# A narrower scope for the scan's priority, a priority for the split of weights, and two small buffer edits

## The chip, the cores and the metric

The kernel runs on one core of a Trainium2 chip. Its engines are TensorE (PE; the loading of its stationary operand is listed apart as PEld), VectorE (DVE), ScalarE (ACT), GpSimd (POOL) and SyncE (SP), whose queue issues the DMAs here. The metric is the device time of one execution in microseconds: before the change 2582.29 us, the median of three runs (2581.88 to 2584.9).

## The reference, cut to what matters

Two layers over 2048 tokens of width 1024, everything in float32: a Mamba-2 layer (SSD) and a sliding-window attention layer with sinks. Each is norm, one input projection, mixer, gate, one output projection, norm, residual. The part of the Mamba layer that the change touches is the chunked scan, with 8 groups of 4 heads, a state of 128 and chunks of 128 tokens:

```python
seg = a_cs[..., :, None] - a_cs[..., None, :]
decay = jnp.exp(jnp.where(causal, seg, -jnp.inf))
cb = jnp.einsum('bclgn,bcsgn->bcgls', Cc, Bc)
y_diag = jnp.einsum('bcgrls,bcsgrp->bclgrp', cb[:, :, :, None] * decay, x)
states = jnp.einsum('bclgn,bcgrl,bclgrp->bcgrpn', Bc, decay_to_end, x)
...
y_off = jnp.einsum('bclgn,bcgrpn,bcgrl->bclgrp', Cc, h_in, jnp.exp(a_cs))
```

## The kernel before, in words

**Products.** Every large product runs as three matmuls on operands that are split into a rounded high part and the remainder: high·high, low·high and high·low (`mm3`, L88). A block of weights (128 columns, all 1024 rows) is split in `split_w` (L143): a DMA brings `wraw`, ACT copies it to `whi`, POOL subtracts to get `wlo`. Each of the three tiles has two buffers, so the block after next can only be split when the products of an earlier one are done with its buffers. The same function splits the gate weights of the attention layer.

**Stages.** The Mamba layer goes through the tokens in two halves of 1024. In a half, the loop over the 8 groups runs `ssm_proj` (L665): six blocks of weights (B, C, x0, x1, z0, z1), each multiplied with two blocks of 512 tokens, 24 matmuls a product; behind each product ACT evicts it and DVE and ACT apply the convolution and the SiLU. The scan of the group before (`ssm_scan`, L756) is interleaved into these products: `interleave` (L49) advances it in 19 steps over a group. The scan of the half's first group can't start before `dt_proj` (L588) has made the half's tables; it comes with the second group. After the last group the scan runs beside the first pieces of the output projection. Then the output projection, the attention layer (head groups of 4 query heads, two halves of tokens) and its output projection follow.

**The scan.** `stage1` (L770) works on one chunk. PE transposes x and B and multiplies B with C; DVE and ACT make `xd`, `bh`, `bl`, `xw`, `xh`, `xl` (the operands of the state products) and `cbm`, the masked scores; then four ACT Relu and an exponential make the decays `dec` from `ab` (the row sums, broadcast by a DMA), another exponential and a product on POOL turn `ab` into `ce`, and DVE multiplies `dec` by `cbm`. The steps of the scan are: stage1 of chunks 0 and 1, then for each pair of chunks the state products (`sps`) and the carrying of the state, stage1 of the next two chunks, and the output products (`yt`, L847), which read `xd`, `dec`, `ce` and the states.

**The order on the engines.** The program text isn't the order of execution. A planner goes through the instructions with estimated durations and gives each engine, at each moment, the ready instruction that stands first in the text; a tile that has no free buffer makes its first writer not ready. `high_priority(offset=n)` moves the instructions of its block n places forward in this ranking. Each engine then executes its list in that order and waits on semaphores where something isn't there yet. In `stage1` everything after PE's part has an offset of 60.

**Small tensors at the start.** `ssm_consts` (L554) loads the convolution weights, their bias and the gate norm as `rows`, transposes them on PE and scales them into `cw`, `cb` and `gn`. It stands in the text behind the first whole product of B. The ring `px` has four buffers of 128 x 1024 floats; the x tiles of `prep` (L95, four for each block of 512 tokens) and some scratch of `dt_proj` go through it.

Of the kernel before, what the change touches and what calls it, by code (L numbers as in the profile page):

```python
# [11 lines left out]
F32 = mybir.dt.float32  # L12
F32R = mybir.dt.float32r
I32 = mybir.dt.int32
U32 = mybir.dt.uint32
AF = mybir.ActivationFunctionType
ALU = mybir.AluOpType
# [4 lines left out]
P = 128  # L22
T = 2048
D = 1024
# [36 lines left out]
class Trunk:  # L61
# [81 lines left out]
    def split_w(self, src, cols):  # L143

        nc = self.nc
        kt = src.shape[0] // P
        raw = self.wp.tile([P, kt, cols], F32, tag="wr", name="wraw")
        nc.sync.dma_start(raw, src.rearrange("(k p) c -> p k c", p=P))
        hi = self.wp.tile([P, kt, cols], F32R, tag="wh", name="whi")
        nc.scalar.activation(hi, raw, AF.Copy)  # L150
        lo = self.wp.tile([P, kt, cols], F32R, tag="wl", name="wlo")
        nc.gpsimd.tensor_tensor(lo, raw, hi.bitcast(F32), ALU.subtract)  # L152
        return hi, lo

    def rope_tables(self, wp):
# [398 lines left out]
    def ssm_consts(self, pool):  # L554
        nc, io = self.nc, self.io

        def bcast(ap, n, name):
            t = pool.tile([P, n], F32, name=name)
            nc.sync.dma_start(t, ap.partition_broadcast(P))
            return t  # L560

        self.abc = bcast(io["ssm_a_log"][0], NH, "abc")
        nc.scalar.activation(self.abc, self.abc, AF.Exp)
        nc.vector.tensor_scalar(self.abc, self.abc, -1.0, None, ALU.mult)
        self.dtb = bcast(io["ssm_dt_bias"][0], NH, "dtb")
        d = bcast(io["ssm_d"][0], NH, "dall")
        self.dch = pool.tile([P, NH // 2], F32, name="dch")
        d2 = d.rearrange("p (t two) -> p t two", two=2)
        nc.vector.tensor_copy(self.dch[0:64], d2[0:64, :, 0])
        nc.vector.tensor_copy(self.dch[64:P], d2[64:P, :, 1])  # L570

        self.cw = pool.tile([P, 4, 32], F32, name="cw")
        self.cb = pool.tile([P, 32], F32, name="cb")
        rows = pool.tile([P, 2, P], F32, name="rows")
        nc.sync.dma_start(rows[:, 0, :], io["ssm_conv_w"][0].rearrange("k (t p) -> (k t) p", p=P))
        nc.sync.dma_start(rows[0:32, 1, :], io["ssm_conv_b"][0].rearrange("(t p) -> t p", p=P))
        nc.sync.dma_start(rows[32:48, 1, :], io["ssm_gate_norm"][0].rearrange("(t p) -> t p", p=P))
        pt = self.tp.tile([P, P], F32, tag="tr", name="pt")
        nc.tensor.transpose(pt, rows[:, 0, :], self.ident)
        nc.vector.tensor_scalar(self.cw.rearrange("p k t -> p (k t)"), pt, 0.5, None, ALU.mult)  # L580
        pt = self.tp.tile([P, 48], F32, tag="tr", name="pt")
        nc.tensor.transpose(pt, rows[0:48, 1, :], self.ident[0:48, 0:48])
        nc.vector.tensor_scalar(self.cb, pt[:, 0:32], 0.5, None, ALU.mult)
        nc.vector.tensor_scalar(self.gn, pt[:, 32:48], 0.5, None, ALU.mult)
        self.halo = pool.tile([P, 32, 3], F32, name="halo")
        self.hsave = [pool.tile([P, 256], F32, name=f"hsave{g}") for g in range(NG)]
# [169 lines left out]
    def ssm_scan(self, sp, yp, tabs, hf, g, res, yT):  # L756


        nc = self.nc
        dt, acs, cd, w2, atd = (tabs[k] for k in ("dt", "acs", "cd", "w2", "atd"))  # L760
# [9 lines left out]
        def stage1(c):  # L770
            if c > 7:
                return
            ab = abs_[c]
            s, o = divmod(c, 4)
            sl = slice(o * P, (o + 1) * P)
            x0, x1, Bt, Ct = (res[n, s] for n in ("x0", "x1", "B", "C"))
            pt = (yp.tile([P, 4, P], F32, tag="y", name="pt", bufs=2) if c % 2
                  else self.tp.tile([P, 4, P], F32, tag="tr", name="pt"))
            nc.tensor.transpose(pt[:, 0, :], x0[:, sl], self.ident)
            nc.tensor.transpose(pt[:, 1, :], x1[:, sl], self.ident)  # L780
            last = hf == 1 and c == 7
            if not last:
                nc.tensor.transpose(pt[:, 2, :], Bt[:, sl], self.ident)
            nc.tensor.matmul(pt[:, 3, :], Bt[:, sl], Ct[:, sl], start=True, stop=True)
            with self.tc.high_priority(offset=60):
                xv = pt[:, 0:2, :].rearrange("p a (h d) -> p (a h) d", d=64)
                xd = sp.tile([P, 4, 64], F32, tag="xd", name="xd", bufs=4)
                hb = dt[:, c, 4 * g:4 * g + 4].unsqueeze(2).to_broadcast([P, 4, 64])
                nc.vector.tensor_tensor(xd, xv, hb, ALU.mult)
                bx = None  # L790
                if not last:
                    bh = sp.tile([P, P], F32R, tag="bh", name="bh")
                    nc.scalar.activation(bh, pt[:, 2, :], AF.Copy)
                    bl = sp.tile([P, P], F32R, tag="bl", name="bl")
                    nc.vector.tensor_tensor(bl, pt[:, 2, :], bh.bitcast(F32), ALU.subtract)
                    xw = sp.tile([P, 4, 64], F32, tag="xw", name="xw", bufs=1)
                    hb = w2[:, c, 4 * g:4 * g + 4].unsqueeze(2).to_broadcast([P, 4, 64])
                    nc.vector.tensor_tensor(xw, xv, hb, ALU.mult)
                    xf = xw.rearrange("p h d -> p (h d)")
                    xh = sp.tile([P, 256], F32R, tag="xh", name="xh")  # L800
                    nc.scalar.activation(xh, xf, AF.Copy)
                    xl = sp.tile([P, 256], F32R, tag="xl", name="xl")
                    nc.vector.tensor_tensor(xl, xf, xh.bitcast(F32), ALU.subtract)
                    bx = bh, bl, xh, xl
                cbm = sp.tile([P, P], F32, tag="cbm", name="cbm", bufs=1)
                nc.vector.tensor_tensor(cbm, pt[:, 3, :], self.triu, ALU.mult)
                dec = sp.tile([P, 4, P], F32, tag="dec", name="dec", bufs=4)
                for r in range(4):
                    nc.scalar.activation(dec[:, r, :], ab[:, r, :], AF.Relu, scale=-1.0,  # L809
                                         bias=acs[:, c, 4 * g + r:4 * g + r + 1])  # L810
                ce = None
                if not (hf == 0 and c == 0):
                    ce = ab
                    nc.scalar.activation(ce, ab, AF.Exp)  # L814
                    nc.gpsimd.tensor_tensor(ce, ce, Ct[:, sl].unsqueeze(1).to_broadcast([P, 4, P]), ALU.mult)  # L815
                nc.scalar.activation(dec, dec, AF.Exp, scale=-1.0)
                nc.vector.tensor_tensor(dec, dec, cbm.unsqueeze(1).to_broadcast([P, 4, P]), ALU.mult)  # L817
            sts.append((xd, bx, dec, ce))

        def states(c):  # L820
# [54 lines left out]
        for c in range(4):  # L875
            load(c)
        stage1(0)
        yield
        stage1(1)
        yield  # L880
        hprev = self.hsave[g] if hf else None
        hd = decayed(0, hprev)
        yield
        for c in range(0, 8, 2):
            sps = states(c)
            h0 = hprev
            h1, hd = state(c, sps[:, 0, :], hd)
            yield
            hprev, hd = state(c + 1, sps[:, 1, :], hd)
            stage1(c + 2)  # L890
            yield
            stage1(c + 3)
            yield
            outputs(c, (h0, h1))
            load(c + 4)
            load(c + 5)
            yield
# [161 lines left out]
```

## Time and profile before

| | |
|---|---|
| median of three runs | 2582.29 us |
| the profiled execution | 2584.72 us, span 2583.0 us |
| PE busy | 2527.8 us (98%) |
| DVE busy | 1673.7 us (65%) |
| ACT busy | 1274.9 us (49%) |
| POOL busy | 921.6 us (36%) |
| mean granted TensorE clock | 0.995 |
| DMA | 224.46 MB, 87 GB/s mean |

The profile is one execution. Its span runs from the first to the last instruction; the execution's own time has 1.7 us around it. The granted clock is TensorE's as a share of full speed: 1.00 is 2.4 GHz, and a window that lies wholly at the lower level, 1.2 GHz, would show 0.50. Matmuls overlap in the pipeline: one is listed with 0.39 us while the next starts 0.23 us after it. Where PE is busy throughout and at full clock, the time of a stretch is set by PE alone.

### The profile page before, as it was taken

To read this page: it belongs to the slowest core of one execution; us is meant where nothing else is said; L and a number is where in the kernel's file an instruction comes from. 1 tells how busy PE (TensorE), PEld (TensorE's weight loads), DVE (VectorE), ACT (ScalarE), POOL (GpSimd) and SP (SyncE) were. 2 spreads that over 40 slices of the span, in tenths; PEclk is the share of its full clock that TensorE was granted. 3 is DMA by queue.
4 is the path that set the end of the run, shared out by engine and by line. 5 is a ranking of instruction groups with operands and counts; after the bars stand their busy time and mean duration, and the time that the engine had idled before them with its cause. 6 is when DMAs were issued, how large, how long until landed. Compare 5 with 4: busy or idle time off the path is not lost.

```text
span 2583.0 us, 38760 instructions
## 1 busy us (share of the span) xinstructions
PE 2527.8 (98%) x14083; PEld 2107.9 (82%) x14083; DVE 1673.7 (65%) x3363; ACT 1274.9 (49%) x3195; POOL 921.6 (36%) x817
## 2 busy tenths in 40 slices
PE   7999999999999999999999999999999999999998
PEld 6878888888777888888887888888888888888787
DVE  6677666766776667666678544447777777767422
ACT  5455555555645555555566422324554455545321
POOL 2344444444434454444445222222222112220222
PEclk9999999999999999999999999999999999999999
DMA  4332223223423222222325332234111121111343
GB/s 127 96 86 64 81 76 87 74 70 78 116 62 105 78 83 77 78 78 78 82 78 174 113 101 90 90 128 140 54 54 58 54 78 54 54 32 58 123 146 120
DMA packets 266656, 224.46 MB, mean 87 GB/s; under 512 B 31136, under 2 KB 229984, under 8 KB 266464
## 3 DMA queue, kind: packets, MB, share of 16 engines
q1 hardware_dynamic: 266464, 221.98, 29.2%
q8 instruction: 111, 1.82, 0.3%
q14 instruction: 81, 0.66, 0.1%
HBM read 179.72 MB, written 42.21 MB: 86 GB/s over the span
## 4 chain that ended last, share of the span: by engine, by line
PE 74%; DVE 10%; POOL 5%; DMA 4%; ACT 4%; issue 4%; SPq 0%; POOLq 0%; ACTq 0%; DVEq 0%
PE u L251 19%; PE ps L90 14%; PE ps L92 14%; PE ps L91 14%; DVE sx L749 2%; DMA ab<-atd 2%; POOL wlo L152 2%; PE sc L420 2%; PE yt L856 2%; PE yt L861 1%; PE ot L474 1%; PE ot L478 1%; DVE dec L817 1%; PE tt L453 1%; POOL ab L815 1%
## 5 line engine op out<-in xcount | busy, mean ns | idle before, releaser
L90 PE MATMUL ps<-hi,whi 128*128 128x512 f32 (+1 forms) x1808 | 725.5, 401 | 9.4 <-ACT whi L150 4.7
L92 PE MATMUL ps<-hi,wlo 128*128 128x512 f32 (+1 forms) x1808 | 706.1, 391 | 4.2 <-POOL wlo L152 4.2
L91 PE MATMUL ps<-lo,whi 128*128 128x512 f32 (+1 forms) x1808 | 704.6, 390 | 0.2 <-DVE lo L140 0.2
L92 PEld LDWEIGHTS ps<-hi,wlo 128*128 128x128 f32 x1808 | 340.7, 188 | 80.2 <-POOL wlo L152 6.1
L90 PEld LDWEIGHTS ps<-hi,whi 128*128 128x128 f32 x1808 | 341.2, 189 | 77.9 <-issue 15.9
L152 POOL TENSOR_TENSOR wlo<-wraw,whi 128x1024 fp32r<-128x1024 f32 x114 | 282.6, 2479 | 319.1 <-ACT whi L150 310.6
L749 DVE SCALAR_TENSOR_TENSOR sx<-raw,cw,sx 128x512 f32<-128x512 f32 x384 | 342.9, 894 | 71.3 <-ACT sx L746 66.5
L91 PEld LDWEIGHTS ps<-lo,whi 128*128 128x128 f32 x1808 | 341.6, 189 | 55.2 <-DVE lo L140 0.8
L251 PE MATMUL u<-ol,yh 128*128 128x512 f32 x768 | 239.6, 393 | 1.0 <-DVE ol L223 0.9
L251 PE MATMUL u<-oh,yh 128*128 128x512 f32 x768 | 240.5, 394 | 0.0
L251 PE MATMUL u<-oh,yl 128*128 128x512 f32 x768 | 237.6, 391 | 0.0
L809 ACT ACTIVATE dec<-ab,acs 128x128 f32<-128x128 f32 x512 | 165.4, 392 | 128.9 <-DMA ab<-atd 114.3
L815 POOL TENSOR_TENSOR ab<-ab,sx 128x512 f32<-128x512 f32 x120 | 168.9, 1409 | 154.5 <-ACT ab L814 140.5
L752 ACT ACTIVATE raw<-sx 128x512 f32<-128x512 f32 x128 | 80.6, 630 | 221.4 <-DVE sx L749 221.3
L90 PE MATMUL ps<-qh,hi 128*128 128x384 f32 x512 | 181.1, 355 | 0.0
L870 POOL TENSOR_TENSOR ysb<-ysb,zz 128x256 f32<-128x256 f32 x128 | 108.1, 861 | 197.9 <-DVE ysb L868 197.7
L235 POOL TENSOR_TENSOR yl<-yr,yh 128x1024 fp32r<-128x1024 f32 (+1 forms) x64 | 119.3, 1864 | 161.3 <-ACT yh L233 161.2
L233 ACT ACTIVATE yh<-yr 128x1024 fp32r<-128x1024 f32 (+1 forms) x64 | 54.1, 845 | 242.3 <-PE u L251 189.3
L91 PE MATMUL ps<-ql,hi 128*128 128x384 f32 x512 | 172.1, 337 | 0.9 <-POOL ql L332 0.9
L251 PEld LDWEIGHTS u<-ol,yh 128*128 128x128 f32 x768 | 143.9, 188 | 34.3 <-DVE ol L223 2.6
L92 PE MATMUL ps<-qh,lo 128*128 128x384 f32 x512 | 171.9, 336 | 0.0
L251 PEld LDWEIGHTS u<-oh,yl 128*128 128x128 f32 x768 | 144.5, 188 | 31.4
(213 smaller groups left out, 4527.7 us busy)
## 6 DMA issues: line engine op xcount, KB each, us to landing
wraw<-in_ssm_w_in SPq DMA_DIRECT2D x98, 512.0 KB, 4.1
ab<-atd SPq DMA_DIRECT2D x128, 256.0 KB, 4.6
xt<-in_x SPq DMA_DIRECT2D x32, 512.0 KB, 4.8
yT<-ysb SPq DMA_DIRECT2D x64, 256.0 KB, 2.5
yr<-yT SPq DMA_DIRECT2D x32, 512.0 KB, 4.0
xt<-x SPq DMA_DIRECT2D x32, 512.0 KB, 4.0
oraw<-in_ssm_w_out SPq DMA_DIRECT2D x16, 512.0 KB, 5.9
x<-xt SPq DMA_DIRECT2D x32, 256.0 KB, 2.1
```

The source lines that it names most:

```text
L90: nc.tensor.matmul(ps, sh, mh, start=first, stop=False)
L91: nc.tensor.matmul(ps, sh, ml, start=False, stop=False)
L92: nc.tensor.matmul(ps, sl, mh, start=False, stop=last)
L152: nc.gpsimd.tensor_tensor(lo, raw, hi.bitcast(F32), ALU.subtract)
L233: nc.scalar.activation(yh, yr, AF.Copy)
L235: nc.gpsimd.tensor_tensor(yl, yr, yh.bitcast(F32), ALU.subtract)
L251: nc.tensor.matmul(st["u"][h], y[:, k, :], w[:, j, 512 * h:512 * h + 512], start=k0 + k == 0 and m == 0, stop=k0 + k == kt - 1 and m == 2)
L749: nc.vector.scalar_tensor_tensor(sx, raw[:, j:j + BLK], self.cw[:, j, ct:ct + 1], sx, ALU.mult, ALU.add)
L752: nc.scalar.activation(th, sx, AF.Tanh)
L809: nc.scalar.activation(dec[:, r, :], ab[:, r, :], AF.Relu, scale=-1.0, bias=acs[:, c, 4 * g + r:4 * g + r + 1])
L815: nc.gpsimd.tensor_tensor(ce, ce, Ct[:, sl].unsqueeze(1).to_broadcast([P, 4, P]), ALU.mult)
L870: nc.gpsimd.tensor_tensor(yv, yv, res[f"z{pr}", s][:, sl], ALU.mult)
```

## The change

Three edits. The priority block of `stage1` ends behind `cbm`: the decays (Relu, exponentials, the product on POOL and the one on DVE) keep their place in the text but have no lead any more. In `split_w` the ACT copy and the POOL subtraction get a lead of 40; the load doesn't. `cbm` has two buffers, and `rows`, which had a tile of its own, becomes a tile of the ring `px`.

```diff
@@ split_w
-        hi = self.wp.tile([P, kt, cols], F32R, tag="wh", name="whi")
-        nc.scalar.activation(hi, raw, AF.Copy)
-        lo = self.wp.tile([P, kt, cols], F32R, tag="wl", name="wlo")
-        nc.gpsimd.tensor_tensor(lo, raw, hi.bitcast(F32), ALU.subtract)
+        with self.tc.high_priority(offset=40):
+            hi = self.wp.tile([P, kt, cols], F32R, tag="wh", name="whi")
+            nc.scalar.activation(hi, raw, AF.Copy)
+            lo = self.wp.tile([P, kt, cols], F32R, tag="wl", name="wlo")
+            nc.gpsimd.tensor_tensor(lo, raw, hi.bitcast(F32), ALU.subtract)
@@ ssm_consts
-        rows = pool.tile([P, 2, P], F32, name="rows")
+        rows = self.px.tile([P, D], F32, tag="px", name="rows")[:, 0:2 * P].rearrange("p (a b) -> p a b", a=2)
@@ stage1: the block under high_priority(offset=60) ends behind cbm
-                cbm = sp.tile([P, P], F32, tag="cbm", name="cbm", bufs=1)
+                cbm = sp.tile([P, P], F32, tag="cbm", name="cbm", bufs=2)
                 nc.vector.tensor_tensor(cbm, pt[:, 3, :], self.triu, ALU.mult)
-                dec = sp.tile([P, 4, P], F32, tag="dec", name="dec", bufs=4)
-                for r in range(4):
-                    nc.scalar.activation(dec[:, r, :], ab[:, r, :], AF.Relu, scale=-1.0,
-                                         bias=acs[:, c, 4 * g + r:4 * g + r + 1])
-                ...
-                nc.scalar.activation(dec, dec, AF.Exp, scale=-1.0)
-                nc.vector.tensor_tensor(dec, dec, cbm.unsqueeze(1).to_broadcast([P, 4, P]), ALU.mult)
+            dec = sp.tile([P, 4, P], F32, tag="dec", name="dec", bufs=4)
+            for r in range(4):
+                nc.scalar.activation(dec[:, r, :], ab[:, r, :], AF.Relu, scale=-1.0,
+                                     bias=acs[:, c, 4 * g + r:4 * g + r + 1])
+            ...
+            nc.scalar.activation(dec, dec, AF.Exp, scale=-1.0)
+            nc.vector.tensor_tensor(dec, dec, cbm.unsqueeze(1).to_broadcast([P, 4, P]), ALU.mult)
```

## Rows read from the trace of the kernel before

**Rows 1.** The page, part 1: busy time, share of the span, instructions

```profile
PE 2527.8 (98%) x14083; PEld 2107.9 (82%) x14083; DVE 1673.7 (65%) x3363; ACT 1274.9 (49%) x3195; POOL 921.6 (36%) x817
```

**Rows 2.** Busy time by window, middle groups: window, us, engines, PEclk, DMA, GB/s

```profile
840.00:1170.00 330.00, 330.00 (x1954) 272.90 (x1953) 221.02 (x391) 184.72 (x437) 152.05 (x117) 1.00 0.28 77
```

**Rows 3.** Timeline of PE: start us, us, instruction, [idle before <-releaser]

```profile
130.86 0.50 PE L90 MATMUL ps<-hi,whi 128*128 128x512 f32 x1 [2.07 <-ACT whi L150]
133.75 0.80 PE L92 MATMUL ps<-hi,wlo 128*128 128x512 f32 x1 [2.15 <-POOL wlo L152]
...
818.97 0.50 PE L90 MATMUL ps<-hi,whi 128*128 128x512 f32 x1 [2.66 <-ACT whi L150]
821.45 0.66 PE L92 MATMUL ps<-hi,wlo 128*128 128x512 f32 x1 [1.75 <-POOL wlo L152]
```

**Rows 4.** Busy time by window, behind the two stalls

```profile
130.00:135.00 5.00, 1.99 (x5) 1.36 (x6) 4.96 (x8) 3.42 (x8) 2.81 (x1) 0.71 0.03 4
135.00:140.00 5.00, 5.00 (x32) 3.83 (x32) 4.06 (x8) 3.30 (x8) 0.25 (x1) 0.60 0.42 113
...
820.00:825.00 5.00, 3.55 (x20) 2.71 (x22) 5.00 (x8) 2.69 (x6) 2.78 (x2) 0.66 0.40 105
```

**Rows 5.** Timeline of PE: the products of B begin

```profile
103.60 0.40 PE L91 MATMUL ps<-lo,whi 128*128 128x512 f32 x1
103.83 0.39 PE L92 MATMUL ps<-hi,wlo 128*128 128x512 f32 x1
```

**Rows 6.** Timeline of ACT ahead of the two stalls

```profile
115.94 1.27 ACT L809 ACTIVATE dec<-ab,acs 128x128 f32<-128x128 f32 x4
...
122.33 0.62 ACT L814 ACTIVATE ab<-ab 128x512 f32<-128x512 f32 x1
...
129.77 1.04 ACT L150 ACTIVATE whi<-wraw 128x1024 fp32r<-128x1024 f32 x1
...
804.27 1.28 ACT L809 ACTIVATE dec<-ab,acs 128x128 f32<-128x128 f32 x4 [2.68 <-DMA ab<-atd]
...
817.86 1.05 ACT L150 ACTIVATE whi<-wraw 128x1024 fp32r<-128x1024 f32 x1
```

**Rows 7.** Timeline of POOL: wlo in the first stall, and at a group start

```profile
130.88 2.81 POOL L152 TENSOR_TENSOR wlo<-wraw,whi 128x1024 fp32r<-128x1024 f32 x1 [1.88 <-ACT whi L150]
...
171.54 2.38 POOL L152 TENSOR_TENSOR wlo<-wraw,whi 128x1024 fp32r<-128x1024 f32 x1 [0.70 <-ACT whi L150]
```

**Rows 8.** Timeline of DVE at the same group start

```profile
172.16 2.32 DVE L817 TENSOR_TENSOR dec<-dec,cbm 128x512 f32<-128x512 f32 x1
```

**Rows 9.** Who waited for whom, PE: us in total, times, longest

```profile
PE sps L91 <- DVE xl L803: 4.8, 9, 1.4
```

**Rows 10.** Timeline of PE: between the halves, and in the attention layer

```profile
695.72 0.47 PE L779 MATMUL pt<-ident,sx 128*128 128x128 f32 x1 [2.46 <-DVE lo L140]
...
1836.35 0.33 PE L384 MATMUL tq<-ident,qf 128*128 128x128 f32 x1 [0.48 <-POOL qf L374]
```

**Rows 11.** Busy time by window: the last scan

```profile
1350.00:1410.00 60.00, 54.41 (x357) 43.13 (x357) 49.05 (x81) 41.46 (x80) 30.96 (x27) 0.94 0.50 148
```

**Rows 12.** Single lines of the kernel: duration ns min/median/max, first and last start

```profile
L803 DVE TENSOR_TENSOR xl<-xw,xh x120: 406/416/2606, 107.1 to 1395.5; 128x256 fp32r<-128x256 f32 x120
...
L815 POOL TENSOR_TENSOR ab<-ab,sx x120: 1275/1298/2310, 120.3 to 1394.5; 128x512 f32<-128x512 f32 x120
...
L817 DVE TENSOR_TENSOR dec<-dec,cbm x128: 669/685/2848, 118.8 to 1398.1; 128x512 f32<-128x512 f32 x128
```

**Rows 13.** Timeline of SP: the first load of rows

```profile
16.45 0.43 SPq L575 DMA_DIRECT2D rows<-in_ssm_conv_w  x1
```

**Rows 14.** Timeline of PE: transposes of x and of rows

```profile
27.95 0.60 PE L136 MATMUL pt<-ident,xt 128*128 128x128 f32 x4
...
30.73 0.33 PE L579 MATMUL pt<-ident,rows 128*128 128x128 f32 x1 [0.27 <-DVE lo L140]
```

**Rows 15.** The tile rows: its loads, issue to landing

```profile
DMA to landing us min/median/max: 4.1/4.3/4.6
```

More of the change, by code (lines that the diff above doesn't have):

```diff
@@ L804, in stage1 @@
                     bx = bh, bl, xh, xl
-                cbm = sp.tile([P, P], F32, tag="cbm", name="cbm", bufs=1)
+                cbm = sp.tile([P, P], F32, tag="cbm", name="cbm", bufs=2)
                 nc.vector.tensor_tensor(cbm, pt[:, 3, :], self.triu, ALU.mult)
-                dec = sp.tile([P, 4, P], F32, tag="dec", name="dec", bufs=4)
-                for r in range(4):
-                    nc.scalar.activation(dec[:, r, :], ab[:, r, :], AF.Relu, scale=-1.0,
-                                         bias=acs[:, c, 4 * g + r:4 * g + r + 1])
[L811 to L815, printed above, removed]
-                nc.scalar.activation(dec, dec, AF.Exp, scale=-1.0)
-                nc.vector.tensor_tensor(dec, dec, cbm.unsqueeze(1).to_broadcast([P, 4, P]), ALU.mult)
+            dec = sp.tile([P, 4, P], F32, tag="dec", name="dec", bufs=4)
+            for r in range(4):
+                nc.scalar.activation(dec[:, r, :], ab[:, r, :], AF.Relu, scale=-1.0,
+                                     bias=acs[:, c, 4 * g + r:4 * g + r + 1])
+            ce = None
+            if not (hf == 0 and c == 0):
+                ce = ab
+                nc.scalar.activation(ce, ab, AF.Exp)
+                nc.gpsimd.tensor_tensor(ce, ce, Ct[:, sl].unsqueeze(1).to_broadcast([P, 4, P]), ALU.mult)
+            nc.scalar.activation(dec, dec, AF.Exp, scale=-1.0)
+            nc.vector.tensor_tensor(dec, dec, cbm.unsqueeze(1).to_broadcast([P, 4, P]), ALU.mult)
             sts.append((xd, bx, dec, ce))
```

## The prediction

> **What bounds the kernel now.** I read the shares first: PE is busy 98% of the span, the next engine (DVE) 65% [rows 1]. So the time is TensorE's, and an edit that only reorders work can win back no more than PE's idle time, 2583.0 − 2527.8 = 55 us, plus what a lowered clock costs behind idle stretches. Then I cut the span into windows. In the middle of a half of the scan phase PE is busy 330.00 us of 330, at full clock, while ACT, DVE and POOL have slack [rows 2]: in these groups no reordering can gain anything. Last I went through PE's timeline for its idle pieces. Two pairs stand out, each in the first group that follows the dt tables of a half: PE waits for the high part of a weight and then for its low part, 2.07 + 2.15 us at 131 us and 2.66 + 1.75 us at 819 us [rows 3]. Behind both the granted clock falls to its lower level, 1.2 instead of 2.4 GHz [rows 4].
>
> Why the split is late there can be read off ACT. The weights of x0 take the buffers of B's, which are free when the two products of B have run. These begin just before 103.60, and a matmul starts every 0.23 us [rows 5]; 48 of them and half a microsecond of transposes put their end at about 115. The copy `whi` on ACT starts at 129.77 [rows 6]. In between ACT works off the decays of four chunks, which the scan's priority of 60 has put ahead: per chunk four Relu (1.27 us together), the exponential of `ab` and that of `dec` (0.62 each, they have one shape) [rows 6], 2.5 us, for the four chunks 9.4 (the very first chunk has no `ab` exponential). At 819 us it is the same, and worse: ACT first sits idle 2.68 us for the broadcast of `ab`, with the decays at the head of its queue, and `whi` comes at 817.86 [rows 6]. In the other groups the decays come two at a time and the stalls don't exist.
>
> **The change part by part.** No instruction is added or removed; the order on ACT, DVE and POOL changes, one buffer is added and one tile moves.
>
> *Decays behind, split ahead.* First stall: idle 2.07 + 2.15 = 4.22. Clock: a mean of 0.71 over 130 to 135 and 0.60 over 135 to 140 [rows 4] is 2 × 0.29 × 5 = 2.9 us and 2 × 0.40 × 5 = 4.0 us at the half level; taken as one piece ending at 139.0 it began at 132.1, and PE worked in it from 133.75, so 5.25 us at half pace, 2.6 lost. Together 6.8. Second stall: 2.66 + 1.75 = 4.41; 0.66 over 820 to 825 is 3.4 us at the half level, all of it worked through, 1.7 lost; together 6.1. The ceiling is 12.9 us.
>
> How much of it comes back depends on where the planner puts `whi`. If it runs as soon as its buffers are free, at 115.9, it is 13 us early, and `wlo` (2.81 us here [rows 7]) too. If the decays of the first three chunks, traced before it, still precede it (1.9 + 2.5 + 2.5) with some 2.7 us of the convolution's own evictions, it starts at about 125.5, ends at 126.6, and `wlo` ends at 129.4; PE wants the one at 128.8 (130.86 − 2.07) and the other at 129.5. So even the worse order almost suffices in the first stall. In the second, where the buffers of B are free at about 803 and `whi` may go into the very gap in which ACT waits for `ab`, it is 14 us early. I take 5.5 of 6.8 and 6.0 of 6.1: −11.5; the ends are 0 and −12.9.
>
> What is behind the decays now? Their consumers on PE are the output products, five scan steps later in program order; a group's twelve products of 24 matmuls are 66 us at the pace of [rows 5], a group has 19 steps, and five of them are over 17 us, against a chain (four Relu, two exponentials, 1.3 us on POOL, 0.7 on DVE [rows 6, 12]) of under 5. I count the delay of the decays at nothing. That cover is missing only in the last scan, whose steps run beside the first output pieces: there PE is already idle 60 − 54.41 = 5.6 us and the clock at 0.94 costs another 3.6 [rows 11]. I take 0 for it, with −5 (xl no longer behind a decay product) and +5 (the output products wait as long again as now) as ends.
>
> *DVE: xl ahead of the decay product.* PE waits for `xl` nine times, 4.8 us in all [rows 9]. At the start of a group the product of `dec` runs just before `xl` and takes 2.32 us instead of its median 0.69, ending after the `wlo` on POOL that began before it, and `xl` comes behind both [rows 7, 8, 12]; this place recurs, at 417, 499, 580, 662, 1185 and 1265 us, seven in all. With the decays at normal priority `xl` goes first. Were it to start at 172.2 unhindered it would win 2.3 us. But an `xl` itself has taken up to 2.61 us against a median of 0.42 [rows 12]; I take that row: the delay passes to it, and the win is what the product runs on after `wlo`, 0.56 us, at the three or so of the seven places where PE waits: −1.5, ends 0 and −4.8.
>
> The Trainium skill, "SBUF — State Buffer", section "Who interferes with whom", says that a DVE instruction with two SBUF inputs and a GpSimd instruction that reads SBUF shut each other out, the first holding the shared port to its end. The rows agree: the product began 0.62 us after the `wlo` and ended 0.56 us after it [rows 7, 8]. By this rule `xl` in front is blocked just the same and this part is −1.5; without it, it would be all of −4.8.
>
> *Two buffers for cbm.* One buffer makes the next masked scores wait for the previous chunk's decay product. That product is now late and cbm still early, so the second buffer only keeps the old order possible. No wait on cbm shows before: 0.
>
> *Transition between the halves.* At 695.72 a transpose waits 2.46 us [rows 10] for a bank that an ACT copy frees late, behind a Relu and an exponential. Moving these behind could save 0.3 + 0.6 us by [rows 6]; the copy also stands behind an instruction that waits for its load. 0, ends −4 and +2.
>
> *Attention.* The split's priority holds here too. At each of the six later changes of head group a transpose waits about 0.5 us for the small copy of `qf` on POOL, which stands behind `wlo` [rows 10] (one of the six rows). An earlier `wlo` clears that, or meets a DVE instruction instead: −1, ends −3 and +4.
>
> *`rows` in the px ring.* The ring has four buffers and `rows` is its ninth user, after both blocks' eight x tiles. The first x tile of the second block is read until 28.55, when its last transposes end [rows 14]. So the loads of `rows`, which were issued from 16.45 on, go out at about 28.6 and land 4.1 to 4.6 us later, as they did before [rows 13, 15]: at 33, against the transpose at 30.73 [rows 14]. That makes the convolution weights some 2.5 us late. PE has projection work and three more x transposes to do meanwhile, if the planner sees the delay; if the three loads wait at the head of SP's queue, the next weight load behind them waits too. +1, ends 0 and +5.
>
> **Sum.** −11.5 − 1.5 − 1 + 1 = −13.0. The profiled execution took 2584.7 us (span 2583.0 and 1.7 around it), 2.4 above the median of 2582.29. It would become 2571.7, which at the median is 2569.3; I say 2570.
>
> **Rivals.**
> (a) *The gain is handed back.* PE comes 6 us earlier to work that hangs on DVE, and DVE is busy 4.96 of 5 us from 130 on and 4.06 of the next 5 [rows 4]. For it: PE's waits for `xl` lie right behind such stretches. Against it: the decay products leave DVE's head just there. If three quarters of −13 go, 2579 (2577 to 2587).
> (b) *The split doesn't get ahead.* A lead of 40 instructions isn't much where a product alone has 24 matmuls and each scan chunk some 19 instructions; the decays of three chunks stay in front, a `wlo` behind two `ab` products on POOL (1.3 us each [rows 12]) loses another 2.6, and half of each stall remains, with its low clock: −6, 2576 (2573 to 2581).
> (c) *Slower: wlo in the way of xl.* An earlier `wlo` on POOL stretches the DVE instruction beside it by up to 2.2 us (2.61 − 0.42 [rows 12]). Where that is `xl`, the state products wait as soon as their slack is used up, and nine times it is used up now [rows 9]. If one `xl` in each of the fourteen later groups loses 1.6 us net, that is +22, against −13 from the rest: +9, 2591 (2588 to 2600). It decides from about 0.9 us per group on. Against it: only nine of 120 `xl` are waited for now, and the number of `wlo` doesn't change.
> The rule of the Trainium skill ("SBUF — State Buffer", "Who interferes with whom") speaks for (c): whichever starts first holds the port for its whole length.
> (d) *More than forecast.* The last scan and the transition gain as well (−5 and −4): 2560 (2555 to 2563).
>
> **Chances.** Forecast (2563 to 2577) 0.50; (d) 0.08; (b) 0.13, half of it beyond 0.2%; (a) 0.15; (c) 0.14. A measurement of this kernel tells 0.2% (5.2 us) from no change: faster means below 2577.1, slower above 2587.5. Faster 0.50 + 0.08 + 0.06 = 0.64; same 0.07 + 0.15 = 0.22; slower 0.14. The range for 8 in 10 runs from 2558 (most of (d)) to 2587, which leaves out (c) and the far edge of (d).
>
> **What would show it.** Right: PE's waits for `whi` and `wlo` at about 131 and 819 us are gone, the clock stays at full there, `whi` stands before the third or fourth chunk's Relu on ACT, and PE's busy time plus idle falls by 11 to 14 us with the middle groups unchanged at about 82 us. (a) would show as new PE waits for `xl` or `hn` at 135 to 180 and 825 to 860 us; (b) as shorter waits in the old places; (c) as idle PE in the middle groups, ahead of the state products, with an `xl` of over 2 us beside a `wlo`. The step of `rows` is wrong if PE's first projection pauses by more than 1 us between 28 and 40 us. The forecast is wrong if the two stalls go and the time doesn't follow.

## The result: slower by about 27 us, and the profile after

2609.9 us (median of 4 runs) against 2582.6 for the kernel before on the same chip: ratio 1.0107, 95% interval 1.0089 to 1.0124. The forecast was 2570. Both forecast stalls went, and more than twice their worth was lost elsewhere in the scan phase. The profiled execution is the shortest of the four after the change (2607.6 us), so the accounts below add up to 22.9 us and not to 27.

Page, part 1, of the changed kernel (engine, busy us, share, instructions):

```profile
PE 2533.3 (97%) x14083; PEld 2107.7 (81%) x14083; DVE 1702.6 (65%) x3363; ACT 1275.1 (49%) x3195; POOL 928.1 (36%) x817
```

The span is 2605.9, 22.9 longer: PE's idle time grew by 17.4 to 72.6 us, its busy time by 5.5 [rows 1]. Line numbers from L149 on are one higher than before (in some experiments by one or two more). Who waited for whom, on PE (us in total, times, longest):

```profile
PE sps L91 <- DVE xl L804: 17.1, 26, 2.5
PE sps L90 <- ACT xh L802: 10.8, 13, 1.5
...
PE ps L92 <- POOL wlo L153: 3.8, 4, 1.7
```

The waits for `xl` grew from 4.8 [rows 9] to 17.1 us, those for `xh` from 2.4 to 10.8. PE's timeline where the stalls were, behind them, and in a middle group:

```profile
129.25 0.50 PE L92 MATMUL ps<-hi,wlo 128*128 128x512 f32 x1 [0.36 <-POOL wlo L153]
136.44 0.39 PE L90 MATMUL sps<-xh,bh 128*128 128x256 f32 x1 [1.22 <-ACT xh L802]
137.75 0.58 PE L91 MATMUL sps<-xl,bh 128*128 128x256 f32 x1 [0.92 <-DVE xl L804]
...
176.08 0.39 PE L90 MATMUL sps<-xh,bh 128*128 128x256 f32 x1 [1.47 <-ACT xh L802]
...
342.36 0.38 PE L90 MATMUL sps<-xh,bh 128*128 128x256 f32 x1 [1.47 <-ACT xh L802]
343.11 0.39 PE L91 MATMUL sps<-xl,bh 128*128 128x256 f32 x1 [0.36 <-DVE xl L804]
...
832.39 0.38 PE L91 MATMUL sps<-xl,bh 128*128 128x256 f32 x1 [2.55 <-DVE xl L804]
```

Of the four stalls [rows 3] 0.36 us is left at 129.25, and nothing of the two at 819; the rest of the 3.8 us for `wlo` lies elsewhere, at 673.92 (1.49), 1371.87 (1.71) and one more place. But PE now waits for the operands of the state products `sps`, in the first groups and in the middle ones. Windows (us, engines' busy times, PEclk, DMA, GB/s): the first two answer to [rows 4], the last is a middle group:

```profile
130.00:135.00 5.00, 5.00 (x41) 3.96 (x40) 4.96 (x6) 2.71 (x9) 2.19 (x2) 1.00 0.53 161
...
820.00:825.00 5.00, 5.00 (x37) 4.05 (x37) 4.66 (x9) 4.52 (x13) 4.38 (x3) 1.00 0.26 66
...
994.00:1079.00 85.00, 82.56 (x479) 67.39 (x478) 57.26 (x97) 45.89 (x108) 37.25 (x29) 1.00 0.27 75
```

In these two windows the clock is full again; in the middle group PE now stands idle for 2.4 of 85 us, against 0 of 330 before [rows 2].

Where the 22.9 us lie is best seen from the distance on PE's timeline between one scan's first output product `yt` and the next scan's, in us (group 1 begins at the first of all; "rest" is from scan 15 on). The last four columns are of experiments that follow: late decays at the start of each half's first scan alone, then the changed kernel with `ab` issued by ACT, without POOL's product, and with three cures together:

```
                    before   after  first scan  ab by ACT  no product  best version
to the first yt      135.8   130.4       129.6      129.5       129.7        129.3
group 1               84.3    88.9        90.8       89.5        83.6         87.7
groups 2 to 7        501.5   510.5       500.9      500.4       499.7        498.4
group 8              101.7    94.3        96.0      102.7        93.4         97.7
group 9               81.9    86.8        86.9       82.2        81.9         83.1
groups 10 to 14      403.1   418.4       402.6      402.6       402.6        402.6
rest                1274.7  1276.6      1277.2     1275.1      1275.0       1275.4
span                2583.0  2605.9      2583.9     2582.0      2565.8       2574.2
```

Before to after: −5.4 and −7.4 at the stalls, together −12.8; +4.6 and +4.9 in the groups right behind them; +9.0 and +15.3 in the eleven middle groups; +1.9 in the rest.

One middle group shows how. Timelines of several engines, before (times; `pt` are the transposes of chunk 6):

```profile
316.91 2.55 POOL L152 TENSOR_TENSOR wlo<-wraw,whi 128x1024 fp32r<-128x1024 f32 x1 [4.38 <-ACT whi L150]
319.49 0.37 SPq L148 DMA_DIRECT2D wraw<-in_ssm_w_in  x1
319.95 1.01 SPq L767 DMA_DIRECT2D ab<-atd  x2
324.83 1.57 ACT L809 ACTIVATE dec<-ab,acs 128x128 f32<-128x128 f32 x5 [3.27 <-DMA ab<-atd]
326.94 0.27 PE L779 MATMUL pt<-ident,sx 128*128 128x128 f32 x1
327.00 1.29 POOL L815 TENSOR_TENSOR ab<-ab,sx 128x512 f32<-128x512 f32 x1 [4.75 <-ACT ab L814]
332.35 0.41 DVE L789 TENSOR_TENSOR xd<-pt,dt 128x256 f32<-128x256 f32 x1
339.86 0.41 DVE L803 TENSOR_TENSOR xl<-xw,xh 128x256 fp32r<-128x256 f32 x1
340.12 0.28 PE L90 MATMUL sps<-xh,bh 128*128 128x256 f32 x1
340.33 0.39 PE L91 MATMUL sps<-xl,bh 128*128 128x256 f32 x1
```

and the same group after:

```profile
318.53 2.38 POOL L153 TENSOR_TENSOR wlo<-wraw,whi 128x1024 fp32r<-128x1024 f32 x1 [4.74 <-ACT whi L151]
320.94 0.37 SPq L148 DMA_DIRECT2D wraw<-in_ssm_w_in  x1
321.40 1.01 SPq L768 DMA_DIRECT2D ab<-atd  x2
326.44 1.57 ACT L810 ACTIVATE dec<-ab,acs 128x128 f32<-128x128 f32 x5 [3.43 <-DMA ab<-atd]
327.50 0.27 PE L780 MATMUL pt<-ident,sx 128*128 128x128 f32 x1
330.33 1.42 POOL L816 TENSOR_TENSOR ab<-ab,sx 128x512 f32<-128x512 f32 x1 [6.63 <-ACT ab L815]
330.52 1.78 DVE L750 SCALAR_TENSOR_TENSOR sx<-raw,cw,sx 128x512 f32<-128x512 f32 x1
333.73 1.29 POOL L816 TENSOR_TENSOR ab<-ab,sx 128x512 f32<-128x512 f32 x1
334.13 1.43 DVE L754 SCALAR_TENSOR_TENSOR sx<-raw,sx 128x512 f32<-128x512 f32 x1
335.49 0.41 DVE L790 TENSOR_TENSOR xd<-pt,dt 128x256 f32<-128x256 f32 x1
337.71 2.62 DVE L804 TENSOR_TENSOR xl<-xw,xh 128x256 fp32r<-128x256 f32 x1
```

In both kernels the load of `ab` stands on SP behind a `wraw` that goes out when the last `wlo` ends (319.46, 320.91), and ACT stands 3.3 and 3.4 us with the Relu at the head of its queue until `ab` lands. Before, the second `xl` ended at 340.27 and PE took it at 340.33, 0.06 us later; this matmul starts 0.21 us behind the one before it, where the earlier ones of the same set come 0.11 to 0.12 apart. So the group had no time to spare at all, which "330.00 of 330" didn't show: the matmul before is listed until 340.40, so that no idle time appears. After, `xd` comes 8.0 us behind the transposes instead of 5.4. Of these 2.6 us, 1.05 are the Relu's (1.1 us ahead of the transposes instead of 2.1), and 1.5 arise between Relu and `xd` (9.05 instead of 7.52): the exponential of `ab` now runs behind the projection's evictions, so POOL's product begins 2.8 us behind the transposes instead of 0.06, and falls beside a convolution step on DVE that takes 1.78 us instead of 0.75. The next chunk's product falls beside a second DVE step (L754, 1.43 us against a median of 0.69), which now also stands ahead of `xd`. The second chunk's `xh` and `xl` are late by as much, and PE waits 1.47 + 0.36 us.

The other middle groups show the same: on average `xd` of chunk 6 comes 5.8 us behind its transposes before and 7.5 after in groups 2 to 7, and 6.5 and 9.0 in groups 10 to 14.

### The profile page after: what moved, and what is told of

Its sections match the earlier page's. It is cut to its first block, busy times and chain, and to the rows that moved or that the text cites. A ratio compares the mean times of both kernels' runs of the same rounds, so it can differ in the third digit from the quotient of the medians.

```text
span 2605.9 us, 38770 instructions
## 1 busy us (share of the span) xinstructions
PE 2533.3 (97%) x14083; PEld 2107.7 (81%) x14083; DVE 1702.6 (65%) x3363; ACT 1275.1 (49%) x3195; POOL 928.1 (36%) x817
## 4 chain that ended last, share of the span: by engine, by line
PE 46%; DVE 10%; POOL 5%; issue 5%; ACT 4%; DMA 3%; SPq 0%; POOLq 0%; ACTq 0%; DVEq 0%
PE u L252 19%; PE ps L90 7%; PE ps L92 6%; PE ps L91 6%; DMA ab<-atd 2%; DVE sx L750 2%; PE sc L421 2%; POOL wlo L153 2%; POOL ab L816 1%; PE ot L475 1%; DVE dec L818 1%; PE ot L479 1%; DVE xl L804 1%; PE tt L454 1%; POOL ysb L871 1%
```

## The experiments

**The parts one by one.** The scope alone (split without its lead), the split's lead alone, the buffers alone, and late decays in chunks 0 to 3 of each half's first scan alone ("first scan alone" from here on):

```diff
 # scope alone: of the change without
-        with self.tc.high_priority(offset=40):      (split_w)
 # first scan alone: the decays' block of the changed kernel under
+            with self.tc.high_priority(offset=60) if g or c > 3 else nullcontext():
```

> The decays behind and the two buffers, the split of weights without a lead. Theory A (the decays' late place alone makes the loss: exponential and product of ab fall among the scan's vector work of every group): about 2608 us (2600 to 2613); the two stalls of 4.2 and 4.4 us at 131 and 819 us are gone, the groups between are 1 to 5 us longer. Rival B (the split's lead puts wlo in front of xl): about 2570 us, waits of PE for xl below 6 us in all.

> The kernel before with the lead of 40 for the split alone. Theory A: 2582 us (2578 to 2586), since a lead of 40 doesn't take whi past decays that have 60; the stalls at 131 and 819 us stay. Rival B (wlo in the way of xl): 2590 us or more, waits of PE for xl 10 us or more in all.

> The kernel before with the second buffer for cbm and rows in px. Theory A and rival B: 2582 to 2584 us, at most 1 us more at the start. If the buffers make the loss: 2600 us or more.

> The decays stay behind only in chunks 0 to 3 of the first scan of each half, elsewhere they have their lead of 60 again; the split keeps its lead of 40. Theory A: the two stalls go (-12.8 us) and the middle groups keep their time, so 2571 us (2568 to 2578); waits of PE for xl and xh near 5 and 3 us in all as before. Rival B (the split's lead does the harm): 2590 us or more.

Scope alone: 2614.0 us, ratio to before 1.0113 [1.0097, 1.0128]; its groups 2 to 7 take 511.4. Split alone: 2584.3, 1.0000 [0.9991, 1.0010]. Buffers: 2586.9, 1.0007 [0.9998, 1.0017]. So the decays' late place makes the whole loss and the split's lead none of it. But the scope alone doesn't take the stalls away (waits for `whi` 5.6, for `wlo` 7.5 us in all): that part of theory A was wrong, the gain of 12.8 needs both edits. In the kernels with the split alone and the buffers alone the stalls stay, too (first `yt` at 134.9 and 135.1), and yet group 1 takes 87.0 and 88.1 us against 84.3 before. First scan alone: 2586.1, 1.0004 [0.9995, 1.0014], where I expected 2571. The middle groups are as before and the first `yt` comes 6.2 us early, but group 1 gives 6.5 back; in the second half group 8 gains 5.7 and group 9 gives back 5.0. The kernel's timelines there:

```profile
154.99 0.37 SPq L148 DMA_DIRECT2D wraw<-in_ssm_w_in  x1
155.46 1.00 SPq L768 DMA_DIRECT2D ab<-atd  x2
159.02 0.27 PE L780 MATMUL pt<-ident,sx 128*128 128x128 f32 x1
160.82 1.57 ACT L811 ACTIVATE dec<-ab,acs 128x128 f32<-128x128 f32 x5 [3.78 <-DMA ab<-atd]
175.70 0.38 PE L90 MATMUL sps<-xh,bh 128*128 128x256 f32 x1 [1.47 <-ACT xh L802]
```

PE is early, but `ab` isn't: the Relu starts 1.8 us behind the transposes.

**Which of the late work.** The lead given back to one chain of the decays each, and `wlo` in four pieces:

```diff
+                with self.tc.high_priority(offset=60):        # ab chain alone
+                    nc.scalar.activation(ce, ab, AF.Exp)
+                    nc.gpsimd.tensor_tensor(ce, ce, Ct..., ALU.mult)
...
+            with self.tc.high_priority(offset=60):            # dec chain alone
+                dec = ...                                     # and its four Relu
+            with self.tc.high_priority(offset=60):
+                nc.scalar.activation(dec, dec, AF.Exp, scale=-1.0)
+                nc.vector.tensor_tensor(dec, dec, cbm..., ALU.mult)
...
+            for k in range(0, kt, 2):                         # wlo in pieces
+                nc.gpsimd.tensor_tensor(lo[:, k:k + 2, :], ..., ALU.subtract)
```

> The changed kernel, with the lead of 60 given back to the exponential of ab and its product alone (ACT and POOL); Relu, the exponential and the product of dec stay late. Theory A1 (the product of ab, pushed into DVE's work on the scan, makes the loss): 2588 us (2580 to 2596), PE's waits for xl and xh below 12 us in all instead of 28. Rival A2 (the dec chain does): 2602 us or more.

> The changed kernel, with the lead of 60 given back to the dec chain alone (four Relu, exponential, product on DVE); exponential and product of ab stay late. Theory A1: 2602 us or more, PE's waits for xl and xh stay above 20 us. Rival A2: 2588 us (2580 to 2596).

> The changed kernel, with wlo as four instructions of 256 columns instead of one of 1024. If a long wlo that holds DVE's xl is the last step of the loss: xl no longer takes 2.6 us but at most 1.2, PE's waits for xl and xh fall from 28 to below 15 us, and the time to 2592 us (2584 to 2600). If the late decays delay xl by DVE's queue alone: 2605 us or more.

> The kernel with the late decays in chunks 0 to 3 of each half's first scan alone, and wlo in four pieces. If wlo's hold on xl is what handed back the gain at 135 to 180 and 825 to 860 us: 2575 us (2568 to 2580). If DVE's work alone did: 2584 us or more.

Lead for the `ab` chain: 2594.3, 1.0030 [1.0016, 1.0045]; waits for `xl` and `xh` 16.5 us instead of 27.9. That is most of the loss, though not down to the 12 us I named. Lead for the `dec` chain: 2636.8, 1.0204 [1.0180, 1.0228], waits 41.4: with Relu and `dec` first, the product is later still (4.2 to 5.4 us behind the transposes of chunk 6 in groups 2 to 7, against 1.8 to 2.9). Both speak for A1. The pieces were a miss: 2663.8, 1.0297 [1.0281, 1.0314], and 2632.0, 1.0179 [1.0164, 1.0194], with the first scan alone late. The timelines of the changed kernel with `wlo` in pieces say why:

```profile
326.88 3.27 POOL L154 TENSOR_TENSOR wlo<-wraw,whi 128x256 fp32r<-128x256 f32 x4 [4.73 <-ACT whi L151]
330.18 0.37 SPq L148 DMA_DIRECT2D wraw<-in_ssm_w_in  x1
330.65 1.00 SPq L769 DMA_DIRECT2D ab<-atd  x2
334.42 0.27 PE L781 MATMUL pt<-ident,sx 128*128 128x128 f32 x1
335.58 1.57 ACT L811 ACTIVATE dec<-ab,acs 128x128 f32<-128x128 f32 x5 [3.93 <-DMA ab<-atd]
```

Four pieces take 3.3 us here (0.88 each on average, 3.5 for four) instead of 2.4, `wraw` and behind it `ab` go out later, and the Relu starts 1.2 us behind the transposes; over the kernel ACT waits 178 us for `ab` instead of 109. I hadn't expected this; it gave theory C.

**`ab` taken out of SP's queue**, in two ways, each with the whole change and with the first scan alone:

```diff
-                nc.sync.dma_start(ab.rearrange(...), ...)
+                nc.scalar.dma_start(ab.rearrange(...), ...)      # ab by ACT
-        nc.sync.dma_start(raw, src.rearrange(...))
+        nc.gpsimd.dma_start(raw, src.rearrange(...))             # or wraw by POOL
```

> The changed kernel, with the broadcasts of ab issued from ACT's queue instead of SP's, where they stand behind a wraw that waits for wlo (157.44 us behind 156.97 in the trace of before). Theory C (late decays hurt because ab lands late and what stands behind the Relu on ACT and DVE is then done in a rush, with POOL's product in it): ACT's idle time ahead of the Relu for the DMA of ab falls from 109 us to below 40, PE's waits for xl and xh from 28 to below 14, the time to 2590 us (2575 to 2597). Rival D (the order alone, wherever ab lands): 2602 us or more.

> The changed kernel, with wraw issued from POOL's queue, so that ab has SP nearly for itself. Theory C: as the one with ab on ACT's queue, 2590 us (2575 to 2600), ACT's idle time for the DMA of ab below 40 us. Rival D: 2602 us or more. If issuing costs POOL much time: above 2610 us, with more POOL time seen.

> Late decays in the first scan's chunks 0 to 3 alone, split with its lead, and wraw issued from POOL's queue. Theory C: the gain of 12.8 us at the two stalls is no longer handed back at 160 to 180 us, where ACT waited 3.8 us for ab: 2572 us (2565 to 2580). Rival D: 2584 us or more.

> Late decays in the first scan's chunks 0 to 3 alone, split with its lead, and ab issued from ACT's queue. Theory C: 2572 us (2565 to 2580). Rival D: 2584 us or more.

With the whole change: 2583.6, 0.9987 [0.9977, 0.9996], and 2586.6, 1.0005 [0.9996, 1.0015]. The loss is gone either way, so the order alone (rival D) doesn't make it. The middle group with `ab` issued by ACT:

```profile
321.01 1.28 ACT L810 ACTIVATE dec<-ab,acs 128x128 f32<-128x128 f32 x4 [0.41 <-DMA ab<-atd]
323.17 0.41 ACT L810 ACTIVATE dec<-ab,acs 128x128 f32<-128x128 f32 x1 [0.89 <-DMA ab<-atd]
325.63 0.27 PE L780 MATMUL pt<-ident,sx 128*128 128x128 f32 x1
326.10 1.79 DVE L750 SCALAR_TENSOR_TENSOR sx<-raw,cw,sx 128x512 f32<-128x512 f32 x1
331.08 0.41 DVE L790 TENSOR_TENSOR xd<-pt,dt 128x256 f32<-128x256 f32 x1
```

In this group it is the same order and the same stretched step, but all of it earlier: Relu 4.6 us ahead of the transposes, `xd` 5.45 behind them, as before. Of the waits for `xl` and `xh` 6.6 us are left. ACT's idle time for `ab` over the kernel hardly fell (109 to 110 and 90 us, where I expected below 40): it waits now where it costs nothing, so that number was a poor test. With the first scan alone late: 2588.0, 1.0012 [1.0003, 1.0022], with `wraw` by POOL, and 2584.4, 0.9997 [0.9987, 1.0006], with `ab` by ACT, not the 2572 expected. So an early `ab` cures the middle groups; in group 1 it doesn't keep the gain (89.5 us), and with `ab` by ACT the stall of the second half is back (group 8, 102.7).

**POOL's product.**

```diff
-                nc.gpsimd.tensor_tensor(ce, ce, Ct..., ALU.mult)
+                pass
```

> The changed kernel without the product of ab with C on POOL (left out of the computation; PE's work stays). Theory A1 (the product among DVE's steps passes the delay on): 2588 us (2578 to 2596), sx steps of 1.4 to 1.8 us in the middle groups shrink to 0.7, PE's waits for xl and xh from 28 to below 14 us. Rival (ACT's order alone): 2602 us or more.

> The kernel before without the product of ab with C on POOL (left out of the computation). The baseline for the one above: 2582 us (2576 to 2585) by either theory, since the middle groups already keep PE busy.

Without it the changed kernel takes 2568.5, 0.9944 [0.9925, 0.9962], and the one before 2573.3, 0.9958 [0.9943, 0.9973]. Nothing of the loss is left, though DVE, SP and PE execute the same instructions in the same order as in the changed kernel, by line and tile, and ACT all but one pair; the intervals of the two overlap. So it is the late product that makes the loss. The middle group of the changed kernel without the product:

```profile
317.99 1.80 ACT L810 ACTIVATE dec<-ab,acs 128x128 f32<-128x128 f32 x5 [2.91 <-DMA ab<-atd]
319.94 0.27 PE L780 MATMUL pt<-ident,sx 128*128 128x128 f32 x1
322.30 0.75 DVE L750 SCALAR_TENSOR_TENSOR sx<-raw,cw,sx 128x512 f32<-128x512 f32 x1
324.88 0.69 DVE L754 SCALAR_TENSOR_TENSOR sx<-raw,sx 128x512 f32<-128x512 f32 x1
325.49 0.42 DVE L790 TENSOR_TENSOR xd<-pt,dt 128x256 f32<-128x256 f32 x1
```

The Relu starts 1.95 us ahead of the transposes, about as before the change, the two steps take 0.75 and 0.69 us, and `xd` comes 5.55 behind the transposes, 7.50 behind the Relu. Over groups 2 to 7 and 10 to 14 `xd` is back at 5.6 and 6.3 us on average. Here the gain at the two stalls is kept, too: group 1 takes 83.6, group 9 81.9 us. The Trainium skill ("SBUF — State Buffer", "Who interferes with whom") says that a DVE instruction with two SBUF inputs contends with a GpSimd instruction that reads SBUF, and that the order of issue decides which of them holds up the other. The trace agrees: the step of 1.78 us began 0.19 behind the product and ended 0.55 behind its end.

**The cures together, and a better version.** The kernel before with `ab` by ACT; the changed kernel with the lead for the `ab` chain and `ab` by ACT; with the product on DVE; and with all three:

```diff
-                nc.sync.dma_start(ab.rearrange(...), ...)
+                nc.scalar.dma_start(ab.rearrange(...), ...)
...
+                with self.tc.high_priority(offset=60):
+                    nc.scalar.activation(ce, ab, AF.Exp)
-                nc.gpsimd.tensor_tensor(ce, ce, Ct..., ALU.mult)
+                    nc.vector.tensor_tensor(ce, ce, Ct..., ALU.mult)
```

> The kernel before, with ab issued from ACT's queue. If an early ab is worth something by itself: 2579 us (2573 to 2582), as in the changed kernel with the same edit, so that the change adds nothing to it. If the late decays keep part of their gain: 2584 us or more here, above the 2583.6 of the changed kernel with this edit.

> The changed kernel, with the lead given back to the exponential and product of ab, and ab issued from ACT's queue. If both cures act on the same delay: 2583 us (2578 to 2587), no better than either the issue alone. If they add up: 2575 us or less.

> The changed kernel with the product of ab with C on DVE instead of POOL. If the product costs by what it does to DVE's steps beside it: about 0.7 us each on DVE in place of a stretch of about 1 us, PE's waits for xl and xh below 14 us, 2578 us (2568 to 2590). If its length in the chain counts, or DVE has no room for 120 more instructions: 2600 us or more.

> The changed kernel with the product on DVE, the lead for ab's exponential and product, and ab issued from ACT's queue. If all three cures act on one delay: 2578 us (2570 to 2586). If DVE has no room in the first groups: 2588 us or more.

An early `ab` gives the kernel before nothing: 2586.7, 1.0014 [1.0004, 1.0023]. Lead for the `ab` chain and `ab` by ACT: 2580.9, 0.9988 [0.9978, 0.9997]; they act on one delay. Product on DVE in the changed kernel: 2594.6, 1.0041 [1.0026, 1.0056], between the two expectations: over half of the loss goes with the hold on DVE's steps; the rest I put down to the 0.79 us that the product takes on DVE itself, which wasn't tried apart. All three: 2576.4, 0.9969 [0.9959, 0.9980], 0.3% faster than the kernel before.

## Why the prediction was wrong

The step that failed: "I count the delay of the decays at nothing." I asked who reads the decays on PE, and found 17 us of cover for the output products. That held in the groups; the output products wait once, 1.5 us in the last scan. What I didn't ask is what else the late work meets on its own engines. It met the scan's chain to `xd`, `xw`, `xh`, `xl`, by POOL's product beside DVE's steps, and that chain's own start hangs on a load that SP issues behind the previous `wlo`. What I had put at nothing cost 24.3 us in the eleven middle groups.

It rested on a reading: "in these groups no reordering can gain anything", from PE's 330.00 of 330 us. True of that window, but I took it as if nothing could be lost there either. Busy time of the bound engine shows no slack; the rows of `xl` and of its matmul do, and in the group shown they stood 0.06 us apart, with PE already held.

The terms one by one. *The two stalls*, −11.5 with a ceiling of 12.9: measured −12.8. The first came by the worse order that I had worked out:

```profile
123.73 1.06 ACT L151 ACTIVATE whi<-wraw 128x1024 fp32r<-128x1024 f32 x1
...
126.35 2.85 POOL L153 TENSOR_TENSOR wlo<-wraw,whi 128x1024 fp32r<-128x1024 f32 x1
```

`whi` stands at 123.73 behind three sets of Relu (I had 125.5), and `wlo` ended at 129.20 (129.4). At the second stall `whi` (817.51) stands behind three sets of Relu, too, not in the gap where ACT waits for `ab`; the stall went all the same. *xl ahead of the decay product*, −1.5: in the middle group a product of `dec` still runs just ahead of the first `xl`, in 0.69 us now, and `xl` takes 2.62 beside `wlo`; the delay passed to `xl` as I had assumed, but the whole chain was 2.2 us late, and the waits grew. The place recurs in the kernel before at 253.57 and 334.90 us, too, which I had left out of the seven. *Buffers*, +1: +2.1 with an interval that holds 0; the loads of `rows` went out at 29.09 as worked out (28.6), but landed in 2.0 us, not in 4.1 to 4.6. *Transition*, 0: PE waits 2.56 us there, against 2.46 [rows 10]. *Attention*, −1: the waits for `qf` are the same 2.5 us in 5 waits, so 0.

The rivals. (a), the gain handed back, came true where I had put it: +4.6 and +4.9 us behind the stalls, by waits for `xh` and `xl` at 136 to 177 and at 832 us. I gave it 0.15 and priced it as the whole outcome; it was only one of two. That PE's earliness is what makes it isn't shown for group 1, since that group grew by 2.7 and 3.8 us with the split alone and the buffers alone, where PE is hardly early (by 0.9 and 0.7 us). (c) had the sight right, idle PE ahead of the state products with an `xl` of 2.6 us beside a `wlo`, and nearly the size (22 us in fourteen groups; +24.3 in eleven). Its cause was wrong: the earlier `wlo` of the split does nothing by itself, and without the split's lead the loss is the same. Nor does the long `xl` beside a `wlo` make the loss: `xl` takes over 2.5 us 7 times before, 19 times after and 20 times in the kernel without the product, which loses nothing. (b) didn't happen. So −12.8 + 9.5 + 24.3 + 1.9 = 22.9 us.

What stays open: why an early `ab` doesn't keep the gain in group 1 while leaving out the product does (DVE at work for 9.8 of 10 us at 170 to 180 after the change speaks for DVE's total work there, but that wasn't tested), and why group 1 grows with the split or the buffers alone; why the stall at 817 us comes back with `ab` issued by ACT (group 8, 102.7); and why the middle groups of the second half lost 3.1 us each and those of the first 1.5 (their `xd` came 2.5 us later instead of 1.8, but what makes that difference wasn't tried).

## What to carry to other kernels

Before work is moved behind other work, look in the stretch where the bound engine is always busy for how early each operand lands before its use; a stretch that is full and whose operands land just in time can only lose. Count what the moved instructions do to their neighbours on their own engines and beside them, not only who reads their results. And look at what stands ahead of a load on its queue: here a load held by another's buffer set the pace of a group, and taking it out of that queue won back the change's loss, though not the gain.

## What the runs showed of the hardware

Four subtractions of 256 columns on POOL took 3.5 us in all where one of 1024 takes 2.5, so cutting an instruction to shorten its hold lengthened the chain behind it. The product of `ab` takes 1.38 us on POOL on average and 0.79 on DVE:

```profile
L816 DVE TENSOR_TENSOR ab<-ab,sx 128x512 f32<-128x512 f32 x120 | 94.8, 791 | 99.3 <-ACT ab L815 99.2
```

This row (groups of instructions: busy us, mean ns) is of the changed kernel with the product on DVE.
